# Thirty-two more tokens of an expert layer through row gathers instead of dense products

## The chip, the cores and the metric

The kernel runs on one core of a Trainium2 chip. A core has five engines that run side by side, each with its own queue: TensorE (PE in the profile; PEld is its weight load), VectorE (DVE), ScalarE (ACT), GpSimd (POOL) and SyncE (SP), which here only issues DMAs. Work passes from one to another by semaphores. The metric is the device time of one execution in microseconds (us); lower is better.

## The reference

One decoder layer for 512 tokens of width 1024. A first half (one combined projection, sliding-window attention, a gated linear recurrence, a gated merge and an output projection) gives `x`; the change touches none of it but for a copy of 32 normalised rows at its end. The second half is a product-key expert layer (PEER):

```
h = rms_norm(x)
q = h @ w_q                                  # 8 heads x 2 x 128
sc = q . keys                                # 128 scores per head and half
top 16 of each half -> 256 sums -> top 16 -> idx (of 16384 experts), gates = softmax
act = gelu(sum_d u[idx, d] * h[d])           # 128 choices per token
out = sum_k gates_k * act_k * v[idx_k]
x = rms_norm(x + out)
```

`u` and `v` are tables of 16384 rows of 1024 float32, 64 MB each. Each token takes 8 x 16 = 128 rows of each.

## The kernel before

Tokens are split into four blocks of 128. Matmuls on float32 data are done in three passes of a rounded "high" part and a "low" remainder (`hi_of` on ACT, a subtraction on DVE; `wload` at line 140, `wsplit` at 148).

**Dense tokens.** Tokens 128 to 511 (384 of them, `DT`) go through all experts. For each chunk `c` of 128 experts, `act_chunk` (627) loads 512 KiB of U into one of three buffers, splits it, and runs 24 matmuls of 384 columns (lines 633, 634, 636); ACT's gelu (638) writes the result to a buffer that is kept until the chunk's V step. There are `KEEP` = 24 + 16 + 10 = 50 such buffers, so up to 50 chunks can be done ahead. In the V step of the expert loop the kernel loads 512 KiB of V into one of two buffers (`v_load`, 877, loads two steps ahead), multiplies the gelu by the gates G (`w`, 905), splits both, and runs 18 matmuls of 512 columns (lines 918 to 920): three token blocks as weights, two halves of the width, three passes. They accumulate in six PSUM banks over all 128 chunks.

**G** is the matrix of gates, zero where an expert was not chosen. It is built from one-hot rows of the routing's indices, two matmuls of 128 columns per token (line 863), in slabs of 32 tokens: 12 slabs. Each slab is written to DRAM (`Gd`, line 869), and the expert loop reads it back by groups of four chunks (`g_load`, 884).

**Sparse tokens.** The first 128 tokens, one per partition, take no part in this. For each of their 128 choices `gather` (663) fetches one row of U per partition by an indirect DMA on POOL (line 666, 512 KiB, four buffers), and `sparse` (670) multiplies it with the token's row `h20` and sums on DVE (line 673). After a gelu, 128 more gathers fetch the rows of V, and line 683 adds them, scaled, into two accumulators in turn.

**Order.** The U chunks are handed out by `fill`: 24 during routing (`F1`, line 806), two before G, then one after every fifth bank of G as long as fewer than `KEEP - HELD` = 43 are done, and the rest after G (line 889). In the expert loop each step of the first 78 makes one new U chunk and uses one V chunk; the last 50 steps have no U chunk left. `pace` (687) spreads the 256 gathers over the steps: a step with a U chunk counts two shares, one without counts one, and the last two steps (`TAILC`) none, so `whole` = 2 x 78 + 48 = 204. A sparse pass follows its gather by two (`GLAG`). The instructions are written in this order, and the framework's planner lays down each engine's own order in advance: what it expects to be ready first goes first, in program order among equals. In the trace, U loads written after the last G write stand ahead of it on SP. Once laid down, each queue runs strictly in order, and an instruction that waits holds up all behind it. The end (after the loop) adds the residual, normalises four blocks and writes them.

Of the kernel before, what the change touches and what calls it, by code (L numbers as in the profile page):

```python
# [9 lines left out]
I32 = mybir.dt.int32  # L10
# [16 lines left out]
NE = 128  # L27
DB = NB - 1
DT = DB * P
# [9 lines left out]
LOOK = 24  # L39
LATE = 16  # L40
# [6 lines left out]
HELD = 7  # L47
TL = 2
# [4 lines left out]
def host(inp):  # L53
    g = {k: np.asarray(v) for k, v in inp.items()}
    A = np.ascontiguousarray
    w = g["w_in"][0]
    o = np.cumsum([0, 512, 128, 128, 512, 512, 512, 512, 1024, 1024])
    aq, ak, av, hq, hf, hi, hg, ga, gh = [w[:, o[i]:o[i + 1]] for i in range(9)]
    aq = aq.reshape(D, AKV, AG, HD).transpose(0, 2, 1, 3).reshape(D, 512)

    def fm(m):
        return m.reshape(KD, P, m.shape[1] // P, P).transpose(2, 1, 0, 3)

    def tm(m):
# [15 lines left out]
    const = np.concatenate(  # L80
        [np.eye(P, dtype=np.float32), tri, later, dist,
         np.full((P, P), 1.0 / P, np.float32),
         np.broadcast_to(np.repeat(np.arange(TK, dtype=np.float32), NB), (P, TK * NB)),
         np.broadcast_to(np.repeat(np.arange(P, dtype=np.float32), QT), (P, P * QT))], 1)
# [23 lines left out]


def layer(nc, tc, a, out, probe=None, upto=99):  # L110
# [69 lines left out]
    NPT = DT // TG  # L180
    Gd = dr.tile([NE // GC, P, NPT, GC * TG], F32, name="Gd")


    with tc.tile_pool(name="front", bufs=1) as fr, tc.tile_pool(name="psf", bufs=1, space=PSUM) as psf:
# [363 lines left out]
        def norm2(n):  # L548
# [62 lines left out]
    with tc.tile_pool(name="peer", bufs=1) as pp, tc.tile_pool(name="psp", bufs=1, space=PSUM) as psp, ExitStack() as ps:  # L611
# [4 lines left out]
        extra = [e8([P, 5, DB, P]) for _ in range(2)]  # L616
        extra = [t[:, i] for t in extra for i in range(5)]

        def gel_tile(c):
            i = c % KEEP  # L620
            if i < LOOK:
                return pp.tile([P, DB, P], F32, tag="gel", bufs=LOOK, name=nm("gel"))
            if i < LOOK + LATE:
                return cur["gel2"].tile([P, DB, P], F32, tag="gel2", bufs=LATE, name=nm("gel"))
            return extra[i - LOOK - LATE]

        def act_chunk(c, eng=None):
# [3 lines left out]
            t = slice(P, S)  # L631
# [6 lines left out]
            ACT.activation(g, o.rearrange("p (g t) -> p g t", t=P), AF.Gelu)  # L638
# [12 lines left out]
        idx0 = pp.tile([P, PH * TK], I32, name="idx0")  # L651
        gta = pp.tile([P, NB, PH * TK], F32, name="gta")
        gate0 = gta[:, 0, :]
        i12 = pp.tile([P, 2, NB, PH * TK], F32, name="i12")
        act0 = pp.tile([P, PH * TK], F32, name="act0")
        wt0 = pp.tile([P, PH * TK], F32, name="wt0")
        iok = pp.tile([P, P, QT], F16, name="iok")
        axt = e8([P, 2, D])
        ax = [axt[:, i, :] for i in range(2)]
# [3 lines left out]
        def gather(i):  # L663
            t = cur["late"].tile([P, D], F32, tag="ga", bufs=GB, name=nm("ga"))
            src, j = (a["un"], i) if i < P else (a["v"], i - P)
            tc.keep_in_program_order(POOL.indirect_dma_start(  # L666
                out=t, out_offset=None, in_=src, in_offset=bass.IndirectOffsetOnAxis(ap=idx0[:, j:j + 1], axis=0)))
            gq.append(t)

        def sparse(i):  # L670
            t = gq.pop(0)
            if i < P:
                V.scalar_tensor_tensor(cur["scr"], t, 1.0, h20, op0=OP.mult, op1=OP.mult, accum_out=act0[:, i:i + 1])  # L673
                if i == P - 1:
                    ACT.activation(act0, act0, AF.Gelu)
                    V.tensor_tensor(wt0, act0, gate0, op=OP.mult)
            else:
                j = i - P
                x_ = ax[j % 2]
                if j < 2:  # L680
                    V.tensor_scalar(x_, t, wt0[:, j:j + 1], None, op0=OP.mult)
                else:
                    V.scalar_tensor_tensor(x_, t, wt0[:, j:j + 1], x_, op0=OP.mult, op1=OP.add)  # L683
# [3 lines left out]
        def pace(goal, after):  # L687
            while nga[0] < min(goal, 2 * P):
# [7 lines left out]
        with tc.tile_pool(name="win", bufs=1) as wp:  # L696
# [5 lines left out]
            SP.dma_start(iok32, a["const"][:, 6 * P + TK * NB:].rearrange("p (i t) -> p i t", t=QT))  # L702
# [118 lines left out]
            e = w16((P, PH * TK), F32, "e")  # L821
            V.scalar_tensor_tensor(e, i12[:, 0, 0, :], float(NE), i12[:, 1, 0, :], op0=OP.mult, op1=OP.add)
            ACT.activation(idx0, e, AF.Copy)
# [4 lines left out]
        with tc.tile_pool(name="gb", bufs=1, reuse_waits="tile") as gp:  # L828
# [4 lines left out]
            for n in range(DB):  # L833
                t = slice(n * P, (n + 1) * P)
                b = bank((P, 4, P))
                for w in range(2):
                    PE.transpose(b[:, w, :], i12[:, w, n + 1, :], ident)
                PE.transpose(b[:, 2, :], gta[:, n + 1, :], ident)
                ACT.activation(iT[:, :, t], b[:, 0:2, :], AF.Copy)
                ACT.activation(gs[:, t], b[:, 2, :], AF.Copy, scale=GS)  # L840
# [33 lines left out]
        acc = [[bank() for _ in range(2)] for _ in range(DB)]  # L874
        vraw = {}
# [13 lines left out]
        fill(KEEP - nu[0])  # L889
        g_load(0)  # L890
        for c in range(VPRE):
            v_load(c)

# [4 lines left out]
        for c in range(NE):  # L898
# [6 lines left out]
            V.scalar_tensor_tensor(w.rearrange("p (s t) -> p s t", t=TG), gel.pop(c).rearrange("p n (s t) -> p (n s) t", t=TG),  # L905
# [6 lines left out]
            if c < NE - TL or c == NE - 1:  # L912
                for tb in range(DB):
                    t = slice(tb * P, (tb + 1) * P)
                    for i, whi, wlo, vh, vl in ready:
                        for hf in range(2):
                            d = slice(hf * 512, (hf + 1) * 512)
                            PE.matmul(acc[tb][hf], whi[:, t], vh[:, d], start=i == 0, stop=False)  # L918
                            PE.matmul(acc[tb][hf], whi[:, t], vl[:, d], start=False, stop=False)  # L919
                            PE.matmul(acc[tb][hf], wlo[:, t], vh[:, d], start=False, stop=i == NE - 1)  # L920
# [3 lines left out]
            if c == NE - 8:  # L924
                yt = [e8([P, 2, D]) for _ in range(2)]
                ys = [yt[n // 2][:, n % 2, :] for n in range(NB)]
                for n in range(NB):
                    SP.dma_start(ys[n], xs_[n])
                gf = h20
                SP.dma_start(gf, a["gfin"].to_broadcast([P, D]))  # L930
            pace(2 * P * share / whole, last.ins)

        while nsp[0] < 2 * P:
            sparse(nsp[0])
            nsp[0] += 1
        ld = exp_ln_set()
        for n in range(NB):
            y = ys[n]
            if n == 0:
                V.tensor_tensor(ax[0], ax[0], ax[1], op=OP.add)  # L940
            sq = s4([P, D])
            s2_ = oc.tile([P, 2], F32, tag="s2_", bufs=4, name=nm("s2_"))
            for hf in range(2):
                d = slice(hf * 512, (hf + 1) * 512)
                V.tensor_tensor(y[:, d], y[:, d], acc[n - 1][hf] if n else ax[0][:, d], op=OP.add)
                ACT.activation(sq[:, d], y[:, d], AF.Square, accum_out=s2_[:, hf:hf + 1])
            r = oc.tile([P, 1], F32, tag="ss", bufs=8, name=nm("rs"))
            V.tensor_tensor(r, s2_[:, 0:1], s2_[:, 1:2], op=OP.add)
            with tc.issue_after(ld):
                ACT.activation(r, r, AF.Ln, bias=epst, scale=1.0 / D)  # L950
                ACT.activation(r, r, AF.Exp, scale=-0.5)
            for hf in range(2):
                d = slice(hf * 512, (hf + 1) * 512)
                V.scalar_tensor_tensor(y[:, d], y[:, d], r, gf[:, d], op0=OP.mult, op1=OP.mult)
                (SP, ACT)[hf].dma_start(out[n * P:(n + 1) * P, d], y[:, d])
# [17 lines left out]
```

## Time and profile before

| | us |
|---|---|
| median of 3 runs | 1702.37 (1698.13 to 1703.45) |
| profiled execution, its own time | 1699.73 |
| its span, first to last instruction | 1698.0 |
| busy in it: PE / DVE / ACT / POOL | 1650.8 / 1258.5 / 726.3 / 409.4 |

Times in the views count from the span's start. An engine's busy time is a sum over the whole span, and says little about which engine sets the pace of a stretch; for that, one looks at what ended the waits there. The granted clock is TensorE's, as a share of 2.4 GHz. Matmuls overlap: a row's duration is longer than the distance to the next one's start, and the distance is what counts.

### The profile page before, as it was taken

The numbers are of one execution on the slowest core, as the hardware profiler recorded it, in microseconds if no ns is written. First come the engines' busy times: TensorE is split into PE (matmuls) and PEld (weight loads), VectorE is DVE, ScalarE is ACT, GpSimd is POOL, SyncE is SP. The second block draws the span as 40 slices with busy tenths as digits, with TensorE's granted clock in tenths as the row PEclk, the third lists the DMA queues.
The fourth block names the chain that finished last, engine by engine and source line by source line (L and its number), as shares of the span: only waits on it lengthen the run. The fifth ranks groups of instructions, "written<-read, shape, count | busy, mean of one in ns | idle before, by whom it ended". The sixth has DMA issues, their size and how long they took to land.

```text
span 1698.0 us, 23371 instructions
## 1 busy us (share of the span) xinstructions
PE 1650.8 (97%) x8571; PEld 1422.9 (84%) x8571; DVE 1258.5 (74%) x2474; ACT 726.3 (43%) x1152; POOL 409.4 (24%) x273
## 2 busy tenths in 40 slices
PE   8999999999999979999799999999999999999997
PEld 6867678888999979998699999999999999887786
DVE  8466653657999977775677777777777777688888
ACT  5433453345455556775233333333333333333334
POOL 4000000000000000000444444444444545443331
PEclk9999999999999989999899999999999999999999
DMA  5311133324333336666978887887888888699895
GB/s 170 112 38 51 50 116 108 124 98 136 123 106 105 107 95 189 206 211 195 345 298 320 301 308 297 319 302 293 315 328 296 311 313 312 225 329 350 308 336 187
DMA packets 146291, 370.81 MB, mean 218 GB/s; under 512 B 11376, under 2 KB 63088, under 8 KB 146176
## 3 DMA queue, kind: packets, MB, share of 16 engines
q1 hardware_dynamic: 107520, 233.11, 40.1%
q0 software_dynamic: 36928, 134.30, 21.1%
q10 hardware_dynamic: 1728, 1.91, 0.4%
q8 instruction: 67, 1.10, 0.3%
q14 instruction: 48, 0.39, 0.1%
HBM read 339.91 MB, written 29.36 MB: 217 GB/s over the span
## 4 chain that ended last, share of the span: by engine, by line
PE 83%; DVE 9%; DMA 4%; ACT 1%; issue 1%; POOL 1%; SPq 0%; DVEq 0%; ACTq 0%; POOLq 0%
PE b L634 9%; PE b L633 9%; PE b L636 9%; PE b L919 9%; PE b L920 9%; PE b L918 9%; PE b L863 5%; PE b L255 5%; PE b L254 5%; PE b L257 5%; DMA vr<-vc 3%; DVE lo L155 2%; POOL sumsq L217 1%; PE b L473 1%; ACT hi L135 1%
## 5 line engine op out<-in xcount | busy, mean ns | idle before, releaser
L666 POOL DMA_INDIRECT ga<-un,idx x128 | 193.9, 1515 | 1005.7 <-issue 783.4
L633 PE MATMUL b<-hT,hi 128*128 128x384 f32 x1024 | 348.2, 340 | 0.8 <-ACT s L603 0.5
L634 PE MATMUL b<-hT,hi 128*128 128x384 f32 x1024 | 347.9, 340 | 0.0
L135 ACT ACTIVATE hi<-s 128x1024 fp32r<-128x1024 f32 (+1 forms) x195 | 206.2, 1058 | 289.2 <-PE b L634 171.6
L918 PE MATMUL b<-hi,whi 128*128 128x512 f32 x768 | 303.4, 396 | 12.0 <-ACT hi L135 12.0
L919 PE MATMUL b<-lo,whi 128*128 128x512 f32 x768 | 304.2, 396 | 6.7 <-DVE lo L155 6.5
L920 PE MATMUL b<-hi,wlo 128*128 128x512 f32 x768 | 303.7, 396 | 0.0
L155 DVE TENSOR_TENSOR lo<-s,hi 128x1024 fp32r<-128x1024 f32 (+1 forms) x195 | 238.7, 1224 | 29.7 <-ACT hi L135 29.0
L666 POOL DMA_INDIRECT ga<-v,idx x128 | 195.5, 1527 | 247.0 <-DVE e L683 228.5
L135 ACT ACTIVATE whi<-w 128x384 fp32r<-128x384 f32 x128 | 67.1, 525 | 374.2 <-PE b L919 336.1
L636 PE MATMUL b<-hT,lo 128*128 128x384 f32 x1024 | 208.1, 338 | 0.0
L910 DVE TENSOR_TENSOR wlo<-w,whi 128x384 fp32r<-128x384 f32 x128 | 71.2, 556 | 179.1 <-ACT whi L135 178.0
L633 PEld LDWEIGHTS b<-hT,hi 128*128 128x128 f32 x1024 | 193.6, 189 | 5.2 <-ACT gel L638 0.7
L634 PEld LDWEIGHTS b<-hT,hi 128*128 128x128 f32 x1024 | 193.6, 189 | 4.1
L918 PEld LDWEIGHTS b<-hi,whi 128*128 128x128 f32 x768 | 145.0, 189 | 42.9 <-ACT hi L135 12.7
L919 PEld LDWEIGHTS b<-lo,whi 128*128 128x128 f32 x768 | 145.2, 189 | 42.2 <-DVE lo L155 12.1
L636 PEld LDWEIGHTS b<-hT,lo 128*128 128x128 f32 x1024 | 178.8, 189 | 0.0
L920 PEld LDWEIGHTS b<-hi,wlo 128*128 128x128 f32 x768 | 144.9, 189 | 33.4
L155 DVE TENSOR_TENSOR lo<-vr,hi 128x1024 fp32r<-128x1024 f32 x128 | 156.3, 1221 | 17.4 <-ACT hi L135 17.0
L683 DVE SCALAR_TENSOR_TENSOR e<-ga,wt,e 128x1024 f32<-128x1024 f32 x126 | 161.0, 1278 | 2.2 <-DMA ga<-v,idx 2.2
L673 DVE SCALAR_TENSOR_TENSOR dscr<-ga,h 128x1024 bf16<-128x1024 f32 x128 | 155.7, 1217 | 3.5 <-DMA ga<-un,idx 3.5
L135 ACT ACTIVATE hi<-vr 128x1024 fp32r<-128x1024 f32 x128 | 134.3, 1049 | 44.5 <-DMA vr<-vc 42.8
(277 smaller groups left out, 2276.5 us busy)
## 6 DMA issues: line engine op xcount, KB each, us to landing
s<-uc SPq DMA_DIRECT2D x128, 512.0 KB
vr<-vc SPq DMA_DIRECT2D x128, 512.0 KB
Gd<-G SPq DMA_DIRECT2D x12, 2048.0 KB
gt<-Gd SPq DMA_DIRECT2D x32, 768.0 KB
s<-wfm SPq DMA_DIRECT2D x30, 512.0 KB
s<-wq SPq DMA_DIRECT2D x16, 512.0 KB
s<-wmg SPq DMA_DIRECT2D x8, 512.0 KB
s<-wout SPq DMA_DIRECT2D x8, 512.0 KB
```

The source lines that it names most:

```text
L135: ACT.activation(dst, src, AF.Copy)
L155: (eng or V).tensor_tensor(lo[:, m], raw[:, m], hi[:, m].bitcast(F32), op=OP.subtract)
L254: PE.matmul(b, wh[:, k, :], rh(i), start=start and i == 0, stop=False)
L633: PE.matmul(o, wh[:, k, :], zh[:, k, t], start=k == 0, stop=False)
L634: PE.matmul(o, wh[:, k, :], zl[:, k, t], start=False, stop=False)
L636: PE.matmul(o, wl[:, k, :], zh[:, k, t], start=False, stop=k == KD - 1)
L666: tc.keep_in_program_order(POOL.indirect_dma_start(out=t, out_offset=None, in_=src, in_offset=bass.IndirectOffsetOnAxis(ap=idx0[:, j:j + 1 ...
L673: V.scalar_tensor_tensor(cur["scr"], t, 1.0, h20, op0=OP.mult, op1=OP.mult, accum_out=act0[:, i:i + 1])
L683: V.scalar_tensor_tensor(x_, t, wt0[:, j:j + 1], x_, op0=OP.mult, op1=OP.add)
L918: PE.matmul(acc[tb][hf], whi[:, t], vh[:, d], start=i == 0, stop=False)
L919: PE.matmul(acc[tb][hf], whi[:, t], vl[:, d], start=False, stop=False)
L920: PE.matmul(acc[tb][hf], wlo[:, t], vh[:, d], start=False, stop=i == NE - 1)
```

## The change

Tokens 128 to 159 (`X` = 32) leave the dense path and are gathered as well. Their 128 choices are laid over the 128 partitions, four choices of each token in one step (`XR` = 4), so that they need 32 gathers of U and 32 of V, as large as the others. 352 tokens stay dense: U matmuls have 352 columns, G has 11 slabs, and the last of the three token blocks has 96 tokens. The gather order is U for the first 128 tokens, U and V for the 32, V for the first 128: 320 in all. Between the two uses of `h20`, POOL loads the 32 tokens' rows into it four times over, from a copy in DRAM (`zX`). The indices and gates of the 32 are moved across partitions by eight small DMAs on SP. The four partial results of each token are added by a matmul with a fold matrix, and these 32 rows are finished inside the loop, at `c` = 122. The sparse results go to one accumulator instead of two in turn. There are 53 gelu buffers instead of 50, each smaller. Of the U chunks done after G, the last three are written after the first V loads in the program.

```
+X = 32
+XR = P // X
+XG = P // XR
+T0 = P + X
+DT = S - T0
...
-LOOK = 24
-LATE = 16
+LOOK = 26
+LATE = 17
...
+LASTU = 3
...
+                if n == 1:
+                    SP.dma_start(zX[:, hf * 512:(hf + 1) * 512], h2[hf][0:X, :])
...
-            t = slice(P, S)
+            t = slice(T0, S)
...
+        sp0, sp1 = Sparse(0, PH * TK), Sparse(1, XG)
+        idxt = pp.tile([P, PH * TK], I32, name="idxt")
+        steps = [(sp0, "un", j) for j in range(sp0.w)] + [(sp1, "un", j) for j in range(sp1.w)] \
+            + [(sp1, "v", j) for j in range(sp1.w)] + [(sp0, "v", j) for j in range(sp0.w)]
+        NS = len(steps)
...
+            if src == "un":
+                V.scalar_tensor_tensor(cur["scr"], t, 1.0, h20, op0=OP.mult, op1=OP.mult, accum_out=b.act[:, j:j + 1])
+                if j == b.w - 1:
+                    ACT.activation(b.act, b.act, AF.Gelu)
+                    V.tensor_tensor(b.wt, b.act, b.gate, op=OP.mult)
+                    if b is sp0:
+                        for r in range(XR):
+                            POOL.dma_start(h20[r * X:(r + 1) * X, :], zX)
+            elif j == 0:
+                V.tensor_scalar(b.ax, t, b.wt[:, j:j + 1], None, op0=OP.mult)
             else:
...
+                V.scalar_tensor_tensor(b.ax, t, b.wt[:, j:j + 1], b.ax, op0=OP.mult, op1=OP.add)
...
+            for n, dst in ((0, sp0.idx), (1, idxt)):
+                e = w16((P, PH * TK), F32, "e")
+                V.scalar_tensor_tensor(e, i12[:, 0, n, :], float(NE), i12[:, 1, n, :], op0=OP.mult, op1=OP.add)
+                ACT.activation(dst, e, AF.Copy)
+            for r in range(XR):
+                p_, c_ = slice(r * X, (r + 1) * X), slice(r * XG, (r + 1) * XG)
+                SP.dma_start(sp1.idx[p_, :], idxt[0:X, c_])
+                SP.dma_start(sp1.gate[p_, :], gta[0:X, 1, c_])
...
-        fill(KEEP - nu[0])
+        fill(KEEP - nu[0] - LASTU)
         g_load(0)
         for c in range(VPRE):
             v_load(c)
+        fill(LASTU)
...
+                    t = slice(tb * P, min(tb * P + P, DT))
+                    m = t.stop - t.start
...
+                            PE.matmul(acc[tb][hf][0:m, :], whi[:, t], vh[:, d], start=i == 0, stop=False)
...
+            if c == NE - 6:
+
+                assert nsp[0] >= NS - sp0.w
+                bs = []
+                for hf in range(2):
+                    bs.append(bank(tag="p"))
+                    PE.matmul(bs[hf][0:X, :], fold[:, 0:X], sp1.ax[:, hf * 512:(hf + 1) * 512], start=True, stop=True)
+                final_rows(yx[0:X, :], [b[0:X, :] for b in bs], P, X)
+            pace(NS * share / whole, last.ins)
```

`final_rows`, called here and for the four blocks at the end, is the end's old code as a function: add the residual, square and sum on ACT, scale, write.

## Rows read from the trace of the kernel before

**Rows 1.** The page, part 1: busy time of each engine.

```profile
PE 1650.8 (97%) x8571; PEld 1422.9 (84%) x8571; DVE 1258.5 (74%) x2474; ACT 726.3 (43%) x1152; POOL 409.4 (24%) x273
```

**Rows 2.** Stretches: busy us (instructions) by engine, granted clock, DMA share, GB/s.

```profile
core 0: us, PE busy (x) PEld busy (x) DVE busy (x) ACT busy (x) POOL busy (x), PEclk, DMA share, GB/s
395.00:597.00 202.00, 201.66 (x1075) 183.22 (x1074) 190.66 (x933) 108.00 (x238) 0.00 (x0) 1.00 0.34 109
610.00:803.00 193.00, 192.67 (x1342) 176.03 (x1340) 145.96 (x220) 131.42 (x145) 0.00 (x0) 1.00 0.61 185
803.00:815.00 12.00, 0.34 (x1) 0.34 (x2) 1.58 (x3) 2.52 (x5) 3.88 (x4) 0.62 0.82 291
812.00:832.00 20.00, 13.97 (x56) 11.55 (x57) 15.61 (x24) 5.91 (x8) 7.08 (x8) 0.73 0.99 375
844.40:1473.00 628.60, 628.60 (x3159) 569.51 (x3158) 466.41 (x608) 228.67 (x302) 298.03 (x188) 1.00 0.83 304
1481.50:1685.30 203.80, 200.45 (x850) 158.97 (x849) 174.07 (x203) 76.38 (x100) 74.11 (x55) 1.00 0.87 310
...
1525.00:1565.00 40.00, 38.59 (x163) 30.06 (x163) 32.91 (x40) 13.86 (x18) 15.08 (x12) 1.00 0.94 343
```

**Rows 3.** Timeline of one paired step: start, us, engine, line, operation, tiles.

```profile
1003.70 1.22 DVE L673 SCALAR_TENSOR_TENSOR dscr<-ga,h 128x1024 bf16<-128x1024 f32 x1
...
1004.61 0.39 PE L918 MATMUL b<-hi,whi 128*128 128x512 f32 x1
...
1004.87 1.23 DVE L155 TENSOR_TENSOR lo<-s,hi 128x1024 fp32r<-128x1024 f32 x1
...
1008.79 0.34 PE L633 MATMUL b<-hT,hi 128*128 128x384 f32 x1
...
1012.98 0.39 PE L918 MATMUL b<-hi,whi 128*128 128x512 f32 x1
```

**Rows 4.** Chain of waits, 1520 to 1565: V loads (first and last of four).

```profile
1522.97 7.48 DMA vr<-vc
...
1551.37 5.26 DMA vr<-vc
```

**Rows 5.** Timeline of PE, 380 to 383: matmuls of 256 columns.

```profile
380.33 0.29 PE L254 MATMUL b<-hT,hi 128*128 128x256 f32 x1
...
382.00 1.12 PE L257 MATMUL b<-hT,lo 128*128 128x256 f32 x8
```

**Rows 6.** Timeline of PE, 640 to 646: a run of G's matmuls.

```profile
641.39 1.82 PE L863 MATMUL b<-oh 128*128 128x128 f16 x14
642.96 0.42 PE L634 MATMUL b<-hT,hi 128*128 128x384 f32 x1
```

**Rows 7.** Timeline, 785 to 850: the way into the expert loop (SPq is SP's queue).

```profile
798.77 0.38 SPq L869 DMA_DIRECT2D Gd<-G  x1
...
801.12 1.55 PE L636 MATMUL b<-hT,lo 128*128 128x384 f32 x8
...
807.58 0.33 SPq L887 DMA_DIRECT2D gt<-Gd  x1
...
814.66 1.65 PE L918 MATMUL b<-hi,whi 128*128 128x512 f32 x3 [11.99 <-ACT hi L135]
```

**Rows 8.** The page, part 5: costly groups (busy us, mean ns, idle before, by whom ended).

```profile
L683 DVE SCALAR_TENSOR_TENSOR e<-ga,wt,e 128x1024 f32<-128x1024 f32 x126 | 161.0, 1278 | 2.2 <-DMA ga<-v,idx 2.2
...
L135 ACT ACTIVATE whi<-w 128x384 fp32r<-128x384 f32 x128 | 67.1, 525 | 374.2 <-PE b L919 336.1
```

**Rows 9.** Timeline, 800 to 830: first gather, its use, and its buffer's next gather.

```profile
808.66 1.02 POOL L666 DMA_INDIRECT ga<-un,idx  x1 [782.21 <-issue]
...
817.26 1.23 DVE L673 SCALAR_TENSOR_TENSOR dscr<-ga,h 128x1024 bf16<-128x1024 f32 x1 [3.47 <-DMA ga<-un,idx]
...
818.76 1.68 POOL L666 DMA_INDIRECT ga<-un,idx  x1 [5.31 <-DVE dscr L673]
```

More of the change, by code (lines that the diff above doesn't have):

```diff
@@ L27 @@
 NE = 128
+X = 32
[3 more added lines that the diff above has]
+DT = S - T0
 DB = NB - 1
-DT = DB * P
 EPS = 1e-6
@@ L180, in layer @@
     NPT = DT // TG
+    zX = dr.tile([X, D], F32, name="zX")
     Gd = dr.tile([NE // GC, P, NPT, GC * TG], F32, name="Gd")
@@ L615, in layer @@
         KEEP = LOOK + LATE + E8S
-        extra = [e8([P, 5, DB, P]) for _ in range(2)]
+        extra = [e8([P, 5, DT]) for _ in range(2)]
         extra = [t[:, i] for t in extra for i in range(5)]
@@ L637, in act_chunk @@
             g = gel_tile(c)
-            ACT.activation(g, o.rearrange("p (g t) -> p g t", t=P), AF.Gelu)
+            ACT.activation(g, o, AF.Gelu)
             gel[c] = g
@@ L671, in sparse @@
             t = gq.pop(0)
[L672 to L676, printed above, removed]
-            else:
[L678 to L683, printed above, removed]
+            b, src, j = steps[i]
+            if src == "un":
[8 more added lines that the diff above has]
+                V.tensor_scalar(b.ax, t, b.wt[:, j:j + 1], None, op0=OP.mult)
+            else:
+                V.scalar_tensor_tensor(b.ax, t, b.wt[:, j:j + 1], b.ax, op0=OP.mult, op1=OP.add)
         nga, nsp = [0], [0]
         def pace(goal, after):
-            while nga[0] < min(goal, 2 * P):
+            while nga[0] < min(goal, NS):
                 gather(nga[0])
@@ L832, in layer @@
             fill(2)
-            for n in range(DB):
-                t = slice(n * P, (n + 1) * P)
+            for n in range(1, NB):
+                f = X if n == 1 else 0
+                t = slice((n - 1) * P - X + f, n * P - X)
                 b = bank((P, 4, P))
                 for w in range(2):
[L837 to L840, printed above, removed]
+                    PE.transpose(b[:, w, :], i12[:, w, n, :], ident)
+                PE.transpose(b[:, 2, :], gta[:, n, :], ident)
+                ACT.activation(iT[:, :, t], b[:, 0:2, f:], AF.Copy)
+                ACT.activation(gs[:, t], b[:, 2, f:], AF.Copy, scale=GS)
                 V.tensor_copy(g16[:, 0, t], gs[:, t])
@@ L874, in layer @@
         acc = [[bank() for _ in range(2)] for _ in range(DB)]
+        fold = late.tile([P, X], F32, name="fold")
+        SP.dma_start(fold, a["const"][:, 6 * P + TK * NB + P * QT:])
         vraw = {}
@@ L892, in layer, with scale_of, final_rows @@
             v_load(c)
+        fill(LASTU)
+        def scale_of(ss, n):
+            r = oc.tile([P, 1], F32, tag="ss", bufs=8, name=nm("rs"))
+            with tc.issue_after(ld):
+                ACT.activation(r[0:n, :], ss, AF.Ln, bias=epst[0:n, :], scale=1.0 / D)
+                ACT.activation(r[0:n, :], r[0:n, :], AF.Exp, scale=-0.5)
+            return r[0:n, :]
+        def final_rows(y, add, t, n):
+            s2_ = oc.tile([P, 2], F32, tag="s2_", bufs=4, name=nm("s2_"))
+            for hf in range(2):
+                d = slice(hf * 512, (hf + 1) * 512)
+                V.tensor_tensor(y[:, d], y[:, d], add[hf], op=OP.add)
+                ACT.activation(cur["scr"][0:n, d], y[:, d], AF.Square, accum_out=s2_[0:n, hf:hf + 1])
+            ss = oc.tile([P, 1], F32, tag="ss", bufs=8, name=nm("rs"))
+            V.tensor_tensor(ss[0:n, :], s2_[0:n, 0:1], s2_[0:n, 1:2], op=OP.add)
+            r = scale_of(ss[0:n, :], n)
+            for hf in range(2):
+                d = slice(hf * 512, (hf + 1) * 512)
+                V.scalar_tensor_tensor(y[:, d], y[:, d], r, gf[0:n, d], op0=OP.mult, op1=OP.mult)
+                (SP, ACT)[hf].dma_start(out[t:t + n, d], y[:, d])
         todo_u = NE - nu[0]
@@ L917, in layer @@
                             d = slice(hf * 512, (hf + 1) * 512)
-                            PE.matmul(acc[tb][hf], whi[:, t], vh[:, d], start=i == 0, stop=False)
-                            PE.matmul(acc[tb][hf], whi[:, t], vl[:, d], start=False, stop=False)
-                            PE.matmul(acc[tb][hf], wlo[:, t], vh[:, d], start=False, stop=i == NE - 1)
+                            PE.matmul(acc[tb][hf][0:m, :], whi[:, t], vh[:, d], start=i == 0, stop=False)
+                            PE.matmul(acc[tb][hf][0:m, :], whi[:, t], vl[:, d], start=False, stop=False)
+                            PE.matmul(acc[tb][hf][0:m, :], wlo[:, t], vh[:, d], start=False, stop=i == NE - 1)
                 ready = []
@@ L924, in layer @@
             if c == NE - 8:
+                ld = exp_ln_set()
                 yt = [e8([P, 2, D]) for _ in range(2)]
                 ys = [yt[n // 2][:, n % 2, :] for n in range(NB)]
-                for n in range(NB):
-                    SP.dma_start(ys[n], xs_[n])
                 gf = h20
                 SP.dma_start(gf, a["gfin"].to_broadcast([P, D]))
-            pace(2 * P * share / whole, last.ins)
-        while nsp[0] < 2 * P:
+                xf = xs_.rearrange("n p d -> (n p) d")
@@ new lines, in layer @@
+                yx = s4([P, D])
+                SP.dma_start(yx[0:X, :], xf[P:T0])
+                for n in range(NB):
+                    t = T0 + (n - 1) * P if n else 0
+                    m = min(P, S - t)
+                    SP.dma_start(ys[n][0:m, :], xf[t:t + m])
+            if c == NE - 6:
+                assert nsp[0] >= NS - sp0.w
+                bs = []
+                for hf in range(2):
+                    bs.append(bank(tag="p"))
+                    PE.matmul(bs[hf][0:X, :], fold[:, 0:X], sp1.ax[:, hf * 512:(hf + 1) * 512], start=True, stop=True)
+                final_rows(yx[0:X, :], [b[0:X, :] for b in bs], P, X)
@@ L934, in layer @@
+            pace(NS * share / whole, last.ins)
+        while nsp[0] < NS:
             sparse(nsp[0])
             nsp[0] += 1
[L936 to L955, printed above, removed]
@@ L956, in layer @@
+        final_rows(ys[0], [sp0.ax[:, 0:512], sp0.ax[:, 512:]], 0, P)
+        for n in range(DB):
+            m = min(P, DT - n * P)
+            final_rows(ys[n + 1][0:m, :], [acc[n][hf][0:m, :] for hf in range(2)], T0 + n * P, m)
     es.close()
```

32 lines of the change are left out of this document (16 added, 16 removed).

## Prediction

> **What bounds the kernel now.** I read the page's busy line first: TensorE (PE) is busy 97% of the span, VectorE (DVE) 74% [rows 1]. That is an average, so I read the stretches next [rows 2]. In routing (395 to 597) PE and DVE are both nearly full: 201.7 and 190.7 of 202 us. While G is built (610 to 803) PE alone is full. From 803 to 815 PE stands still. In the first part of the expert loop, where each step makes one U chunk and uses one V chunk (844 to 1473, "paired" below), PE is never idle. After the last U chunk (1481.5 to 1685.3, "single") it is idle 3.3 us of 203.8, and DMA runs at about nine tenths. The timeline gives a paired step [rows 3]: V's 18 matmuls run from 1004.61 to 1008.79, U's 24 from 1008.79 to 1012.98, 8.37 us together. A single step is 4.18 us of V matmuls; the 48 steps of the stretch took 203.8/48 = 4.25 us. The V buffers explain the difference: on the chain of waits, from one V load's issue at 1522.97 to the one three rounds later at 1551.37, load, ACT's high part and DVE's low part follow one another without a hole; two buffers serve two steps, so such a step is 28.4/6 = 4.73 us [rows 4]. The single part is thus already at the edge of a second limit.
>
> **What the change takes from PE.**
>
> U matmuls narrow from 384 to 352 columns. One costs (1012.98 - 1008.79)/24 = 0.1746 us, V's 512 columns 4.18/18 = 0.2322, the same per column [rows 3]; and 14 matmuls of 256 columns started between 380.33 and 382.00, 0.119 each [rows 5], so a floor, if any, lies under 352's share of 0.160. Gain 24 x 0.0146 = 0.35 us a chunk. The 104 chunks outside routing give -36.3 us. The 24 inside would give 8.4, but DVE has only 11.3 us of idle time in that stretch [rows 2] and keeps its work: between 0 and -8.4, taken -2, since DVE is the nearly full one.
>
> V matmuls gain nothing. The last token block has 96 weight columns instead of 128, but 512 columns still stream.
>
> G loses one of 12 slabs, 64 matmuls. 14 of them took 642.96 - 641.39 = 1.57 us, 0.112 each [rows 6]: -7.2 us, on PE's path since PE is full there. DVE's and ACT's share of the slab lies beside it.
>
> Three more gelu buffers (53 for 50) let three more U chunks be done before the loop. Before, PE finished its last one at about 802.7 and stood until 814.66, while the last G write (issued 798.77) and its load back (807.58) ran [rows 7]. The time that G's 768 matmuls left to U in that stretch was 193 - 768 x 0.112 = 107 us, 8.9 a slab, and nearly all of the 26 chunks due before the loop went there. 11 slabs leave 98 us, room for 98/3.84 = 25.5 of the 29 now due, so about three remain for the hole, 11.5 us. The reordering works against that: if the last three U loads do stand behind V's on SP, they also stand behind the G load, which waits for the G write. Then the hole stays and the chunks come after it. Bounds 0 and -15 (the 12 us, and some of what PE loses after them: its clock, idle before, is granted at 0.73 from 812 to 832, a mix of 1.2 and 2.4 GHz [rows 2]); taken -10, since the U loads have free buffers while SP waits for G and are likely placed first, as the earlier ones were.
>
> Sum of the gains: 36.3 + 2 + 7.2 + 10 = 55.5 us.
>
> **What it adds.** There are 320 gather steps for 256, each moving 512 KiB and one DVE pass. `whole` becomes 2 x 75 + 51 = 201 shares for 204, so a paired step gets 640/201 = 3.18 gathers instead of 2.51, a single one 1.59 instead of 1.25.
>
> DVE: a pass occupies 1.17 us (1003.70 to 1004.87 [rows 3]) or 1.28 for the V rows [rows 8]. A paired step is 466.4/75 = 6.22 us of DVE now, so with 0.67 more passes and narrower w tiles about 6.95 of PE's new 8.02 (3.84 + 4.18). A single one is 174.1/48 = 3.63 now, 3.98 then, of 4.18. DVE becomes tight, but is not the bound. The waits ahead of its narrow passes are back-pressure: ACT waits 336 us in all for PE to release the high-part weights [rows 8].
>
> DMA: a paired step moves U 0.524, V 0.524, G 0.180 and gathers 1.669 = 2.90 MB; at 8.02 us that is 361 GB/s, against 304 now. A single one moves 1.54 MB, 368 GB/s at PE's pace. The trace shows 375 GB/s over 20 us (812 to 832), and 343 over the 40 us in which V loads were late [rows 2]. So neither part can be sure of PE's pace. Bounds of the paired step: 8.02 (PE) and 2.90/0.343 = 8.45. Taken 8.20 (353 GB/s, between the two rates), as here V loads have 8 us a step: 75 x 0.18 = +13.5.
>
> The Trainium skill ("DMA: Bandwidth & Descriptors", Where 436 GB/s comes from) says that for transfers between HBM and SBUF the HBM share of about 358 GB/s binds. The 375 measured here exceeds it, so it is no hard wall for this core alone; by it the steps could not go under 8.10 and 4.30 us, and the part of the sum that is left to DMA would be at least 12 us.
>
> The gathers have four buffers. The first one was issued at 808.66, and its buffer's next one at 818.76: a turn of 10.1 us with DMA nearly full [rows 9]. PE's pace needs a turn of 4 x 8.02/3.18 = 10.1: just enough, inside the 8.20.
>
> Single step: bounds 4.25 (as now) and 5.0 (the V round with longer loads); taken 4.60, near the 4.73 of a binding round, since more gathers share the engines with V: 53 x (4.60 - 4.18) = 22.3, less the 3.5 the old part already lost, +18.8.
>
> Two places inside the loop. (a) After sparse pass 128, `h20` is refilled by four POOL DMAs that wait for that pass; the next gathers stand behind them on POOL and pass 129 waits for their landing. Four issues at about 1 us, and a first gather that took 8.6 us from issue to use (808.66 to 817.26 [rows 9]), bound the DVE stall at 12 us; PE has about one step of prepared work: 0 to +10, taken +3. (b) At c = 122 the 32 rows are folded by PE and normalised: four DVE passes of 0.7 us and two small ones, with ACT between, in the tightest part: 0 to +5, taken +3. The index copies on SP and the row copy zX lie in stretches where DMA is a third busy: 0 (up to +4 if U loads queue behind the index copies). The end after 1685.3 keeps its three blocks: 0.
>
> **Sum.** -55.5 + 13.5 + 18.8 + 6 = -17.2 us on the profiled execution: 1699.7 - 17.2 = 1682.5. The median shown is 2.6 us above that execution, so 1685.
>
> **Rivals.**
>
> Memory keeps up: both parts run at PE's pace, the single part's old 3.5 us come back, and half of the two places is hidden. For it: 375 GB/s was seen, and PE is busy for all 628.6 us of the paired stretch now [rows 2]. -55.5 - 3.5 + 3 = -56: about 1646. If only the V rounds stay as they are, 1667. Against it: 368 GB/s is asked for 221 us on end.
>
> Eaten up: paired steps at 8.40 (345 GB/s), single at 4.75: -55.5 + 28.5 + 26.7 + 6 = +6, 1708.
>
> Slower: the four gather buffers. A turn is POOL issue, transfer, DVE's turn and pass; paired steps follow it as 3.18/4 of the turn. With the other terms kept, it decides from a step of 8.43, a turn of 10.6 us; at 11 the step is 8.76, +55.5 for +13.5: 1727. For it: 10.1 was measured at a full DMA, and DVE passes will queue longer. Against it: that first turn included the cold start.
>
> The change doesn't do what it says: 352 columns cost as much as 384. 38 us of gain go: 1723. Against it: the 256-column row.
>
> **Numbers.** Forecast 0.48 (its own range 1665 to 1700), memory keeps up 0.25, eaten up 0.10, gather turn 0.13, no narrower matmul 0.04. Range 1646 to 1720: it takes in the first rival and most of the second and fourth. A measurement tells about 0.3% (5 us) from no change. Faster: 0.46 + 0.25 + 0.02 = 0.73. Same: 0.02 + 0.08 = 0.10. Slower: 0.17.
>
> **What would show it.** U matmuls of 352 columns 0.160 apart; G built in 11 slabs, about 177 us with the same chunks; PE's standstill before the first V matmul down from 12 us to a few; paired steps of 8.1 to 8.4 us with DMA above 340 GB/s and waits for gathers; single steps near 4.6 with V loads on the chain of waits. It is wrong if paired steps exceed 8.45, if the standstill stays at 12 us, or if single steps stay at 4.2.

## The result, and the profile after

The changed kernel took 1680.96 us (median of 4 runs, 1670.62 to 1686.49), the kernel before 1701.64 in the same comparison: ratio 0.9873, 95% interval 0.9848 to 0.9898. The forecast was 1685, in a range of 1646 to 1720. The profiled execution took 1682.85 us; its span is 1680.8.

The page's busy lines of the changed kernel, which answer to [rows 1]:

```profile
PE 1612.4 (96%) x8511; PEld 1357.3 (81%) x8511; DVE 1316.3 (78%) x2560; ACT 712.5 (42%) x1152; POOL 472.3 (28%) x341
```

PE has 38 us less to do and the span is only 17 us shorter. The stretches of the changed kernel (columns as in [rows 2]) say where the rest went. They are routing, G, the standstill, the paired part and the single part:

```profile
395.00:597.00 202.00, 198.95 (x1094) 181.24 (x1093) 191.67 (x939) 109.25 (x246) 0.00 (x0) 1.00 0.33 110
605.00:790.00 185.00, 182.49 (x1311) 170.13 (x1312) 140.12 (x212) 126.46 (x145) 4.62 (x4) 0.99 0.63 195
790.50:803.20 12.70, 0.05 (x1) 0.00 (x0) 2.33 (x4) 2.37 (x5) 0.00 (x0) 0.66 0.96 335
805.00:1422.80 617.80, 604.69 (x3148) 529.13 (x3149) 523.99 (x703) 223.16 (x301) 338.06 (x243) 0.99 0.95 353
1427.00:1668.00 241.00, 226.15 (x930) 166.11 (x929) 206.41 (x243) 82.58 (x118) 109.04 (x76) 0.99 0.87 315
```

In the paired part PE, never idle before, now stands 13 us, while DMA went from 304 to 353 GB/s. In the single part PE stands 15 of 241 us; before it was 3.3 of 203.8 [rows 2].

The timeline of PE in the changed kernel gives the lengths of the parts (start, duration). The first three rows are one undisturbed paired step, the next three mark the standstill and the second V step, and the last is the first single step:

```profile
1003.93 0.39 PE L972 MATMUL b<-hi,whi 128*128 128x512 f32 x1
1008.12 0.32 PE L642 MATMUL b<-hT,hi 128*128 128x352 f32 x1
1011.92 0.40 PE L972 MATMUL b<-hi,whi 128*128 128x512 f32 x1
...
789.75 0.80 PE L645 MATMUL b<-hT,lo 128*128 128x352 f32 x4
803.22 1.65 PE L972 MATMUL b<-hi,whi 128*128 128x512 f32 x3 [12.67 <-ACT hi L141]
813.91 0.39 PE L972 MATMUL b<-hi,whi 128*128 128x512 f32 x1
...
1422.60 0.40 PE L972 MATMUL b<-hi,whi 128*128 128x512 f32 x1
```

U's 24 matmuls take 1011.92 - 1008.12 = 3.80 us, 0.158 each, and V's 18 take 4.19. An undisturbed step is 7.99 us, but the mean from 813.91 to 1422.60 (74 steps) is 8.226. The kernel before had 77 steps of 8.367 there. The stages side by side, in us. The forecast column regroups the prediction's own terms by where they fall, and misses its sum by 0.3. In it the way from G to the second V step is three more chunks of 4.19, less the 10 of the hole and 7 x 0.35; single steps are 53 x 4.60 + 3 less 50 of the old 4.25:

| stage | before | after | change | forecast |
|---|---|---|---|---|
| start to first G matmul | 613.4 | 611.8 | -1.6 | -2 |
| first to last G matmul | 183.8 | 169.7 | -14.1 | -14.9 (7.2 + 22 x 0.35) |
| last G matmul to first V matmul | 17.5 | 21.7 | +4.2 | with the next, +0.1 |
| first to second V step | 14.2 | 10.7 | -3.5 | |
| second V step to first single step | 644.2 | 608.7 | -35.5 | -34.4 (74 x 8.20 + 3) |
| single steps | 215.7 | 247.9 | +32.2 | with the end, +34.3 |
| end | 9.2 | 10.3 | +1.1 | |
| span | 1698.0 | 1680.8 | -17.2 | -16.9 |

Two waits of the paired part are new. Waits of the changed kernel from 830 to 1400 (engine, tile and line, what ended the wait: us in total, times, longest):

```profile
DVE dscr L695 <- DMA ga<-un,idx: 19.0, 20, 2.0
DVE e L705 <- DMA ga<-v,idx: 11.2, 12, 2.2
PE b L973 <- DVE lo L161: 12.2, 12, 2.0
```

DVE waits for a gather, so the low part of the V rows comes late, and PE waits for that. One such place, with the first V matmul of its step and of the next:

```profile
1026.92 1.22 DVE L695 SCALAR_TENSOR_TENSOR dscr<-ga,h 128x1024 bf16<-128x1024 f32 x1 [1.85 <-DMA ga<-un,idx]
1028.07 1.22 DVE L161 TENSOR_TENSOR lo<-vr,hi 128x1024 fp32r<-128x1024 f32 x1
...
1027.85 0.39 PE L972 MATMUL b<-hi,whi 128*128 128x512 f32 x1
1029.35 0.50 PE L973 MATMUL b<-lo,whi 128*128 128x512 f32 x1 [1.10 <-DVE lo L161]
1037.19 0.39 PE L972 MATMUL b<-hi,whi 128*128 128x512 f32 x1
```

This step took 9.34 us. Such steps are few: `pace` gives most steps three gathers and some four, to make 3.18 in the mean, and in DVE's order 15 of the 74 steps have four sparse passes between their `wlo` and the next. Measured from first V matmul to first V matmul, those 15 lost 17.8 us above 7.97 each, and the other 59 together 1.1, nearly all of it in one step. The rest runs at PE's pace. In the step shown, the gather that DVE waits for was issued at 1018.50 and landed at 1026.83, right behind a group of four passes.

In the single part (1430 to 1660) the wait is another:

```profile
ACT hi L141 <- DMA vr<-vc: 64.4, 33, 5.3
DVE lo L161 <- ACT hi L141: 26.0, 14, 4.1
PEld b L972 <- ACT hi L141: 11.6, 11, 2.4
```

Here ACT waits for the V rows. The chain of waits between 1500 and 1530 has the same round as [rows 4]:

```profile
1501.23 1.23 DVE lo L161
1502.48 6.33 DMA vr<-vc
...
1508.91 1.07 ACT hi L141
1510.00 1.24 DVE lo L161
```

### The profile page after: what moved, and what is told of

It reads as the page before. It is cut to its first block, busy times and chain, and to the rows that moved or that the text cites. A ratio compares the mean times of both kernels' runs of the same rounds, so it can differ in the third digit from the quotient of the medians.

```text
span 1680.8 us, 23572 instructions
## 1 busy us (share of the span) xinstructions
PE 1612.4 (96%) x8511; PEld 1357.3 (81%) x8511; DVE 1316.3 (78%) x2560; ACT 712.5 (42%) x1152; POOL 472.3 (28%) x341
## 4 chain that ended last, share of the span: by engine, by line
PE 60%; DVE 15%; DMA 13%; issue 7%; POOL 3%; ACT 2%; DVEq 0%; ACTq 0%; SPq 0%; POOLq 0%
PE b L973 6%; PE b L974 6%; PE b L972 6%; PE b L642 5%; PE b L645 5%; PE b L643 5%; PE b L891 5%; DMA ga<-un,idx 5%; DMA vr<-vc 5%; PE b L262 4%; PE b L261 4%; DVE lo L161 4%; PE b L264 4%; DMA ga<-v,idx 3%; POOL ga L687 2%
## 5 line engine op out<-in xcount | busy, mean ns | idle before, releaser
L642 PE MATMUL b<-hT,hi 128*128 128x352 f32 x1024 | 330.2, 326 | 1.4 <-ACT hi L141 0.9
L643 PE MATMUL b<-hT,hi 128*128 128x352 f32 x1024 | 331.1, 325 | 0.0
L973 PE MATMUL b<-lo,whi 128*128 128x512 f32 (+1 forms) x768 | 307.6, 401 | 21.6 <-DVE lo L161 21.5
L972 PE MATMUL b<-hi,whi 128*128 128x512 f32 (+1 forms) x768 | 305.4, 399 | 19.1 <-ACT hi L141 18.9
L974 PE MATMUL b<-hi,wlo 128*128 128x512 f32 (+1 forms) x768 | 304.6, 397 | 0.0
L141 ACT ACTIVATE whi<-w 128x352 fp32r<-128x352 f32 x128 | 63.5, 497 | 384.2 <-PE b L973 333.7
L973 PEld LDWEIGHTS b<-lo,whi 128*128 128x128 f32 (+1 forms) x768 | 139.4, 181 | 71.9 <-DVE lo L161 35.7
L645 PE MATMUL b<-hT,lo 128*128 128x352 f32 x1024 | 194.9, 326 | 0.0
L972 PEld LDWEIGHTS b<-hi,whi 128*128 128x128 f32 (+1 forms) x768 | 138.9, 181 | 58.6 <-ACT hi L141 25.0
L974 PEld LDWEIGHTS b<-hi,wlo 128*128 128x128 f32 (+1 forms) x768 | 139.1, 181 | 38.9
L141 ACT ACTIVATE hi<-vr 128x1024 fp32r<-128x1024 f32 x128 | 134.3, 1049 | 65.7 <-DMA vr<-vc 64.4
L262 PE MATMUL b<-hT,hi 128*128 128x512 f32 (+1 forms) x376 | 146.5, 391 | 0.3 <-DVE hT L144 0.3
```

The source lines that it names most:

```text
L141: ACT.activation(dst, src, AF.Copy)
L262: PE.matmul(b, wh[:, k, :], rl(i), start=False, stop=False)
L642: PE.matmul(o, wh[:, k, :], zh[:, k, t], start=k == 0, stop=False)
L643: PE.matmul(o, wh[:, k, :], zl[:, k, t], start=False, stop=False)
L645: PE.matmul(o, wl[:, k, :], zh[:, k, t], start=False, stop=k == KD - 1)
L972: PE.matmul(acc[tb][hf][0:m, :], whi[:, t], vh[:, d], start=i == 0, stop=False)
```

## The experiments

Each kernel is the changed one with one edit, measured against the kernel before on the same chip; ratios are to that one. The expectations count the loop's steps by their means in the changed kernel's profile, 8.23 and 4.68 us. In the profiles of the changed kernel and of the five below that keep its buffers, its gathers and its U width, single steps vary from 4.51 to 4.68, so only what goes beyond that counts.

**Five gather buffers.**

```
-GB = 4
+GB = 5
```

> A fifth gather buffer, nothing else; every engine's order stays as in the changed kernel. Theory R (the turn of the four gather buffers holds the paired steps): DVE's waits for gathers in the paired part (30 us there) nearly vanish, paired steps go from 8.24 to about 8.0 us, the time falls by 12 to 18 us. Theory D (the DMA engines' total rate, 353 GB/s in that part, holds them): the same bytes move no faster, gathers land later instead, paired steps stay within 0.05 us of 8.24 and the time within 5 us. Single steps stay near 4.67 under both.

1663.06 us, ratio 0.9753 (0.9716 to 0.979). The paired step fell to 7.979. The paired stretch and the waits of this kernel from 830 to 1400:

```profile
815.00:1411.00 596.00, 595.35 (x3141) 525.12 (x3140) 517.72 (x698) 223.25 (x301) 341.25 (x242) 1.00 0.97 364
...
DVE dscr L695 <- DMA ga<-un,idx: 3.1, 6, 0.8
```

PE stands 0.65 us instead of 13, and the same bytes now move at 364 GB/s. A gather lands as late as before (median 7.7 us after its issue, 7.5 in the changed kernel). DVE's order again has 15 steps with four passes, but now they lose 1.0 us together. With the same bytes and the same DVE work, it was how many gathers could be under way that made those steps long, and not the transfer rate.

**Three V buffers.**

```
-                vraw[c] = late.tile([P, D], F32, tag="vr", bufs=2, name=nm("vr"))
+                vraw[c] = late.tile([P, D], F32, tag="vr", bufs=3, name=nm("vr"))
```

> A third V buffer with the same look-ahead of two, so that a V load no longer waits for the low part of two steps before; only the order on SP can move. Theory V (the round of load, ACT and DVE over two buffers holds the single steps): ACT's wait for V loads in the single part (61 us) falls below 15, single steps go from 4.67 to 4.25 to 4.35 us, the time falls by 17 to 22 us. Theory D (DMA rate): single steps stay above 4.55, the time falls by less than 6 us. Theory DVE (VectorE's work of about 4 us a step holds them): also above 4.5, with VectorE busy over 92% there.

1672.59 us, ratio 0.9831 (0.98 to 0.9861). Paired steps stayed at 8.217 and single ones fell to 4.351. The single part of this kernel, and the wait that was 64.4 us:

```profile
1430.00:1640.00 210.00, 204.40 (x871) 154.06 (x870) 193.74 (x226) 73.25 (x103) 117.18 (x76) 1.00 0.97 358
...
ACT hi L141 <- DMA vr<-vc: 4.8, 5, 2.1
```

The V round is what held the single part; DMA moves 358 GB/s there once a third load may be out. The profiled execution gained 17 us, as expected, the medians only 8, so the size is less sure than the cause.

**Half the bytes of each gather.** The sums are made from the first half of each row alone.

```
-                out=t, out_offset=None, in_=a[src], in_offset=bass.IndirectOffsetOnAxis(ap=b.idx[:, j:j + 1], axis=0)))
+                out=t[:, 0:512], out_offset=None, in_=a[src].rearrange("n (a d) -> (n a) d", a=2), in_offset=bass.IndirectOffsetOnAxis(ap=b.idx[:, j:j + 1], axis=0)))
...
-                V.scalar_tensor_tensor(b.ax, t, b.wt[:, j:j + 1], b.ax, op0=OP.mult, op1=OP.add)
+                V.scalar_tensor_tensor(b.ax.rearrange("p (a d) -> p a d", a=2), t[:, 0:512].unsqueeze(1).to_broadcast([P, 2, 512]), b.wt[:, j:j + 1],
+                                       b.ax.rearrange("p (a d) -> p a d", a=2), op0=OP.mult, op1=OP.add)
```

> Each gather moves half a row (256 KiB instead of 512), and VectorE reads that half twice, so that its passes stay as long; leaves out: the other half of the gathered rows. If DMA traffic (rate, turn of the buffers or V round) is what the loop loses, both parts run at TensorE's pace: paired 8.0, single 4.2 us, 40 to 45 us less than the changed kernel. If VectorE's 64 more passes are what it loses, the time stays within 8 us of the changed kernel.

1638.68 us, ratio 0.9621 (0.9593 to 0.9649): paired 7.986, single 4.196. DMA issues from 830 to 1400 (KB each, median us from issue to landing), first of the changed kernel:

```profile
vr<-vc SPq DMA_DIRECT2D x70, 512.0 KB, 6.6
...
ga<-un,idx POOLq DMA_INDIRECT x146, 7.5
```

and of this one:

```profile
vr<-vc SPq DMA_DIRECT2D x72, 512.0 KB, 3.3
...
ga<-un,idx POOLq DMA_INDIRECT x145, 4.8
```

With as many DVE passes of the same width, both parts run at PE's pace. Lighter traffic shortens both rounds, and full-width passes on DVE do not keep the steps from PE's pace.

**U matmuls of 384 columns again.**

```
-            o = b[:, :DT]
-            t = slice(T0, S)
+            o = b[:, :S - P]
+            t = slice(P, S)
-            ACT.activation(g, o, AF.Gelu)
+            ACT.activation(g, o[:, X:], AF.Gelu)
```

> The U matmuls take 384 columns again (32 of them unused); all else as in the changed kernel. If the narrower matmul's 44.7 us (128 x 0.35) were gained in full, this costs 40 to 45 us. My theory: routing keeps 2 of its 8.4, and the paired steps only lose what they had above TensorE's pace, 8.24 to about 8.42, so it costs 10 + 2 + 14 = 26 us (20 to 32).

1694.63 us, ratio 0.996 (0.9942 to 0.9979): 14 us slower than the changed kernel, where the 128 chunks have 128 x 0.35 = 45 us more. The way from the last G matmul to the first V matmul in this kernel (784.3 to 805.3):

```profile
784.30:803.50 19.20, 19.20 (x112) 18.90 (x110) 4.48 (x5) 6.70 (x10) 3.50 (x3) 1.00 1.02 352
803.50:805.30 1.80, 0.07 (x2) 0.04 (x1) 1.67 (x3) 1.80 (x4) 0.00 (x0) 1.00 1.03 420
```

Both expectations, 40 to 45 and 20 to 32 us, were too high. Wider chunks fill the way and PE stands 1.7 us; the first V matmul comes only 2.0 us later. G's stretch is as long as with narrow ones (168.6 us): 20 chunks run in it for 22. The paired step is 8.389, near PE's pace with wide U (4.18 + 4.19). So ahead of the loop the narrowing bought a longer standstill, and in the loop 0.16 of its 0.35 us a step.

**The last three chunks pinned behind G.**

```
-                                PE.matmul(b[:, i, :], oh[:, 0, q, :, i], oh[:, 1 + w, q, :, i], start=w == 0, stop=w == 1)
+                                lastg = PE.matmul(b[:, i, :], oh[:, 0, q, :, i], oh[:, 1 + w, q, :, i], start=w == 0, stop=w == 1)
...
+        with tc.issue_after(lastg.ins):
+            fill(LASTU)
...
-        fill(LASTU)
```

> The last three U chunks before the loop are put behind the last G matmul on TensorE; nothing else moves. Theory (the standstill of 12.7 us stayed because the chunks ran ahead of the last G matmul): the last G matmul comes about 11 us earlier (3 x 3.84), the first V matmul 8 to 11 us earlier, the standstill falls under 4 us; 1670 to 1673 us against 1681 for the changed kernel. Rival (the way from G's write to its load lengthens when U loads run beside it): the first V matmul moves by less than 3 us, the standstill stays above 8 us, 1678 to 1682.

1683.56 us, ratio 0.9904 (0.9888 to 0.9921): no gain. Its premise was wrong. Counting U's matmuls gives 28.5 chunks ahead of the first G matmul in both kernels, 21.5 in G's stretch here and 22.3 in the changed one, 3.0 behind it here and 2.3 there: most of the three had been behind G already. The standstill fell to 7.7 us, but the way from the last G matmul to the first V matmul is 21.9 us for 21.7.

**The first gathers held until G's load is back.**

```
-            tc.keep_in_program_order(POOL.indirect_dma_start(
+            if i == 0:
+                gate_.append(POOL.tensor_copy(cur["late"].tile([P, 1], F32, name="gate_"), gts[0][:, 0, 0:1]))
+            with tc.issue_after(gate_[0].ins):
+              tc.keep_in_program_order(POOL.indirect_dma_start(
```

> The first gathers are held on GpSimd until G's first load is back. Theory (four gathers that start ahead of G's write slow it): write to load falls from 13.5 to about 9 us and the first V matmul comes about 4 us earlier; the first loop step then waits for its first gather again and gives 3 us back: 1677 to 1681 us. Rival (the write is slowed by the U loads and not by the gathers): 13 us and the same first V matmul, then 3 us lost: 1683 to 1685.

1683.98 us, ratio 0.9882 (0.9865 to 0.9898). SP's queue in the changed kernel, from G's last write to its first load, and the first gather there:

```profile
783.14 0.38 SPq L897 DMA_DIRECT2D Gd<-G  x1
784.30 9.46 SPq L151 DMA_DIRECT2D s<-uc  x1
793.81 0.42 SPq L904 DMA_DIRECT2D fold<-const  x1
796.69 0.33 SPq L917 DMA_DIRECT2D gt<-Gd  x1
...
779.92 1.02 POOL L687 DMA_INDIRECT ga<-un,idx  x1 [753.04 <-DMA s<-uc]
```

and with the gathers held:

```profile
783.99 0.38 SPq L900 DMA_DIRECT2D Gd<-G  x1
785.14 4.68 SPq L151 DMA_DIRECT2D s<-uc  x1
...
793.43 0.33 SPq L920 DMA_DIRECT2D gt<-Gd  x1
```

Write to load is 9.4 us instead of 13.5 (8.8 before [rows 7]), and 10.8 in the kernel that gathers half the bytes: the four early gathers do slow G's write, and the first V matmul came 2.7 us earlier. But the paired step was 8.393 for 8.226, 12 us over the part. Of these, 8.1 lie in the second V step, which took 16.05 us for 7.94. Its waits, from 800 to 830:

```profile
DVE dscr L698 <- DMA ga<-un,idx: 8.7, 5, 3.1
...
PE b L976 <- DVE lo L161: 5.5, 1, 5.5
```

DVE meets the late first gathers there, PE waits 5.5 us for DVE, and the granted clock is 0.75 behind that wait (816.6 to 826.7), a mix of its two levels. So the theory's mechanism was seen, but what it gave back was 8 us and not 3. Another 3.5 us lie in three steps at `h20`'s refill; why is open.

**Passes of half width.** All bytes are gathered; each pass uses half of its row.

```
-                V.scalar_tensor_tensor(cur["scr"], t, 1.0, h20, op0=OP.mult, op1=OP.mult, accum_out=b.act[:, j:j + 1])
+                V.scalar_tensor_tensor(cur["scr"][:, 0:512], t[:, 0:512], 1.0, h20[:, 0:512], op0=OP.mult, op1=OP.mult, accum_out=b.act[:, j:j + 1])
...
-                V.scalar_tensor_tensor(b.ax, t, b.wt[:, j:j + 1], b.ax, op0=OP.mult, op1=OP.add)
+                V.scalar_tensor_tensor(b.ax[:, 0:512], t[:, 0:512], b.wt[:, j:j + 1], b.ax[:, 0:512], op0=OP.mult, op1=OP.add)
```

> All gathers are moved whole, but VectorE's sparse passes work on half of each row (the other half of each sum is left out). Theory (the loop's loss is the buffers' turns and V's rounds, paced by transfers, not VectorE's time): a pass shorter by 0.55 us shortens the gather buffer's turn by that only, a paired step from 8.23 to 8.0 to 8.15 us and a single one by at most 0.1: 1665 to 1678 us. Rival (VectorE's 64 more passes are what the loop lost): paired steps 7.98 and single ones under 4.3, 1643 us.

1667.13 us, ratio 0.9794 (0.9773 to 0.9816): paired 8.118, single 4.633. The profiled execution, 1674.11 us, was the slowest of the four. In it 7.1 of the 10.9 us that the paired part lost above 7.97 a step lie in three steps at `h20`'s refill (2.2 in the changed kernel). Away from the refill the loss fell from 16.7 us to 3.8. So DVE's time does bear on the paired part: where a step has four passes, six operations of 1024 columns 1.14 us apart and two narrow ones of 0.44 make 7.7 of its 7.97 us, an estimate from the distances of DVE's rows in the changed kernel, and a wait for a gather finds no slack. It is not enough by itself, as five buffers, or half the bytes, reach PE's pace with full passes. In the single part nothing changed.

**Both buffers, 50 chunks ahead of the loop.** Room for the buffers comes from three gelu tiles.

```
-GB = 4
+GB = 5
-LATE = 17
+LATE = 14
-                vraw[c] = late.tile([P, D], F32, tag="vr", bufs=2, name=nm("vr"))
+                vraw[c] = late.tile([P, D], F32, tag="vr", bufs=3, name=nm("vr"))
```

> Five gather buffers and three V buffers, three U chunks fewer ahead of the loop to make room. Theory (two separate buffer limits, one in each part of the loop): paired steps 7.98 us as with five gather buffers, single ones 4.35 as with three V buffers. 78 paired steps for 75 at 7.98 and 50 single ones for 53 at 4.35 against 8.23 and 4.68 is about -26, of which the three chunks cost nothing as they were lost in the standstill: 1650 to 1657 us. Rival (one limit, the transfers as a whole; what one part wins the other gives back): 1662 to 1668, no better than five gather buffers alone.

1651.09 us, ratio 0.9704 (0.9688 to 0.9721): paired 7.988, single 4.253. The two limits are separate and add up. No chunk was left behind G now, and the way to the first V matmul was still 22.6 us (21.7 with 2.3): it is not PE's work that makes it that long.

**Six chunks behind G.**

```
-LASTU = 3
+LASTU = 6
```

and the pinning of the kernel with three.

> Six U chunks are put behind the last G matmul on TensorE. In the changed kernel and in the kernel that pinned three of them there, 22 chunks ran inside G's stretch and three behind it; now 19 and six. Theory (G's stretch is as long as TensorE's own work in it, and the way from G's last matmul to the first V matmul takes about 22 us whatever runs in it): G's stretch 170 to 158 us, the standstill from 12.7 to 1 to 4 us, the first V matmul 8 to 11 us earlier; 1670 to 1674 us against 1681 to 1684. Rival (the stretch is bound by the building of the one-hot tiles on VectorE, or the six chunks' loads stand behind G's write on SP and come late): the stretch stays above 166, or the way behind it grows by as much; first V moves by less than 4 us, 1678 to 1684.

1677.15 us, ratio 0.9871 (0.9847 to 0.9894). The standstill is gone, yet the first V matmul comes at 803.7 us, as in the changed kernel. G's stretch of this kernel, and its waits there:

```profile
611.20:775.20 164.00, 156.76 (x1149) 144.91 (x1149) 129.94 (x192) 115.78 (x125) 0.19 (x1) 0.95 0.61 190
...
PE b L891 <- DVE oh L886: 6.7, 7, 1.2
...
PE b L891 <- DVE oh L885: 0.5, 1, 0.5
```

Against the changed kernel 3.7 chunks (14 us) went out and the stretch fell by 5.7, since PE now waits for DVE's one-hot tiles, 7 us in all, at a granted clock of 0.95, a mix of 2.4 and 1.2 GHz. The way behind G grew to 28.5 us. The rival had the mechanism; the time lies just under its range.

**Both buffers and six chunks behind G.** The edits of the two kernels above together.

> Five gather buffers, three V buffers, and six U chunks behind the last G matmul (50 before the loop). With both buffers and none behind G the way from G to V was 22.6 us of standstill. Theory (nothing of that way needs TensorE): six chunks of 3.84 us fill it, 15 to 20 us earlier than 1651: 1631 to 1636 us. Rival (loads for six chunks lengthen the way to 30 us or more): 1642 to 1648.

1648.05 us, ratio 0.9701 (0.9675 to 0.9727), not to be told apart from 1651.09 and at the upper edge of the rival's range. G's stretch and the two parts of its loop:

```profile
611.70:771.10 159.40, 145.42 (x1078) 134.37 (x1077) 127.28 (x189) 110.76 (x119) 0.40 (x1) 0.88 0.63 185
805.00:1422.40 617.40, 617.27 (x3256) 544.25 (x3255) 531.66 (x709) 231.49 (x312) 346.68 (x245) 1.00 0.97 362
1425.00:1634.00 209.00, 208.16 (x894) 158.79 (x892) 194.44 (x232) 77.98 (x119) 114.11 (x69) 1.00 0.90 336
```

In the loop PE now stands 0.1 us in the first part and 0.8 in the second. What is left is ahead of it: 14 us in G's stretch, with the clock at 0.88 (again a mix of its two levels), and the way behind it, 29.1 us long, which the six chunks now fill.

**The U loads no longer held.**

```
-LASTU = 3
+LASTU = 0
```

> The three U loads are put ahead of the first V loads again (the reordering undone), all else as changed. Theory (the order on SP's queue comes out the same, so this part of the change does nothing): 1678 to 1685 us, standstill 12 to 13.5 us. Rival (the reordering is what cost the standstill): standstill under 8 us, 1672 to 1676.

1681.59 us, ratio 0.9899 (0.9873 to 0.9925); the first V matmul at 803.5 us for 803.2, the last U work ahead of it ending at 790.7 for 790.5. That part of the change does nothing.

## Why the prediction came out right, and where its reasons did not hold

The sum held: -17.2 us was forecast for the profiled execution and -17.2 measured, by stages that each came within about 2 us. That it agrees to the tenth is luck: the four executions of the changed kernel lie 16 us apart. Step by step:

- **U's width** was right as a price (0.158 to 0.160 us a matmul). In the loop it and the price of the gathers are one account: 8.37 to 8.20 was forecast, 8.226 came. Ahead of the loop its 12 us are not to be seen by themselves: with wide U the first V matmul is 2.0 us later.
- **G's stretch** was right in size: a slab of 7.2 us and 22 narrower chunks. But with wide U it is as long (168.6 for 169.7 us, with 20 chunks in it): there the narrowing bought two chunks and no time. Before, after and with wide U the stretch takes 15.3 to 15.4 us a slab.
- **The three held chunks** were right in size and wrong in place. The step that failed was "about three remain for the hole": the standstill stayed at 12.67 us. Three chunks more were done, and from the last G matmul to the second V step only 0.7 us was lost. Of the three, 1.7 ran ahead of G (28.5 there, 26.8 before), and one more ran behind it (2.3 for 1.25). That way grew by 4.2 us as G's write took 13.5 us beside four early gathers; the first loop step gave 3.5 back, as those gathers were already in (with the gathers held, the first two steps take 26.2 us for 18.6). The standstill was the stated sign for this step, so by that sign the step was wrong; the total hid it.
- **Paired steps** were right in size (8.20 forecast, 8.226 measured) and wrong in cause. The prediction laid the 0.18 to a transfer rate between 343 and 375 GB/s. With a fifth gather buffer the same bytes go at 364 GB/s and the step is 7.98. What failed is the step "just enough", which took the turn of the four buffers by the mean number of gathers. The turn, read from the issues of 222 gathers between 830 and 1400, is 10.3 us in the mean: 7.5 from issue to landing, 1.2 of waiting for DVE, 1.2 of the pass, 0.4 to the next issue. At PE's pace the mean step leaves 4 x 7.97/3.18 = 10.0 us for it and a step of three gathers 10.6, but a step of four only 8.0, less than the 9.1 that a turn takes without the waiting; and the loss lies in the steps with four. So the rival of the gather buffers had the mechanism, at its smallest size. That `pace` deals unevenly is read from the trace; no kernel that deals evenly was run.
- **Single steps** were right in both: 4.60 forecast, 4.677 measured, V loads on the chain, and a third V buffer takes most of it back.
- **The two places in the loop** were about right. The two steps around `h20`'s refill took 9.80 and 8.36 us, 1.7 over two mean steps; the step of the fold took 6.11, 1.4 over the mean single step. Each had +3.
- **The end**, costed at nothing, took 1.1 us longer; no experiment touched it.
- **Memory keeps up**, the first rival, is true of memory alone. The Trainium skill ("DMA: Bandwidth & Descriptors", Where 436 GB/s comes from) says that for transfers between HBM and SBUF the HBM share of about 358 GB/s binds. The kernel with both buffers and six chunks moved 362 GB/s over 617 us, with steps of 7.98 and 4.23 us, so no such wall showed here up to PE's pace. Its time, 1648, is also what that rival gave (1646), though it still has its standstills ahead of the loop and other buffers than the rival assumed. Its variant with the V rounds as they are, put at 1667, comes to 1668 by the prediction's own terms; the kernel with five gather buffers is that case, and took 1663.

Open are the size of the V rounds' share (8 us by the medians, 17 by one profile), what the steps at `h20`'s refill cost (0.9 us above PE's pace with five gather buffers, 7.1 with half passes, one profile each), whether dealing the gathers evenly would do what a fifth buffer does, and whether faster one-hot tiles would let the six chunks pay.

## What to carry to other kernels

When a change adds traffic, reckon the turn of each ring of buffers (issue, landing, wait, use) at the landing time under the new load, before a rate in GB/s, and reckon it for the fullest step, not for the mean: here two rings of four and two buffers cost about 30 us (1681 to 1651) while the transfers themselves had room. Work taken off an engine ahead of a fixed chain of write, load and split bought standstill here, not time; look at what ends the chain. And check each stage of a sum separately, as a right total can stand on a wrong step.

## What the runs showed of the hardware that was not expected

- What SP issues next behind G's last 2 MB write can hold its queue for long: a U load for 9.46 us in the changed kernel and 4.68 with the gathers held, the `fold` load of 16 KB for 10.76 us in the kernel with both buffers.
- Landing times follow the load on the DMA engines: a V load of 512 KB lands after 6.6 us in the changed kernel's paired part (353 GB/s) and after 3.3 when the gathers move half their bytes (260 GB/s).
